# RWKV-7 chain of a hybrid block: more chain work issued per product from its launch on, one pause of 5 instead of 9 products, and the group norm issued in two steps

## The chip, the core and the metric

The kernel runs on one core of one Trainium2 chip. The metric is the device time of one execution in microseconds (us), a median over runs. A core has a matrix engine (TensorE, PE), a vector engine (VectorE, DVE), a scalar engine (ScalarE, ACT), GpSimd (POOL) and a queue engine (SyncE, SP). Each takes its own instructions in the order in which they stand in its program and waits for the others through semaphores. Here SP issues the loads of the weights and POOL nearly all other transfers.

## The reference

One block of a hybrid network on 256 tokens of width 2048, in float32. Four branches (a gated linear recurrence a, an attention with forget gates b, a state-space branch c, RWKV-7 d) read a shared input projection; each branch's output of 512 channels goes through its own matrix and is multiplied by a sigmoid gate; the sum goes through an output projection, an MLP with a short convolution, and a last gated projection. Cut to what matters here:

```python
xn = rmsnorm(h, mix_norm[i])
proj = jnp.einsum('bsd,dn->bsn', xn, w_in[i])
...
y_b = forgetting_attention_branch(b_q, b_k, b_v, b_f, ...)
y_d = rwkv7_branch(d_u, rwkv_mu[i], ...)
gates = jax.nn.sigmoid(g_raw.astype(jnp.float32)).reshape(Bsz, S, N_BRANCH, D)
merged = gates[:, :, 0] * jnp.einsum('bsc,cd->bsd', branches[0], w_branch[i, 0])
for j in range(1, N_BRANCH):
    merged = merged + gates[:, :, j] * jnp.einsum('bsc,cd->bsd', branches[j], w_branch[i, j])
```

and of `rwkv7_branch`, the recurrence over tokens and the group norm behind it:

```python
def step(state, inp):
    r_t, w_t, k_t, v_t, kk_t, a_t = inp
    sa = jnp.einsum('bhvk,bhk->bhv', state, -kk_t)
    state = (state * w_t[:, :, None, :] + sa[..., None] * (kk_t * a_t)[:, :, None, :]
             + v_t[..., None] * k_t[:, :, None, :])
    return state, jnp.einsum('bhvk,bhk->bhv', state, r_t)
...
mean = jnp.mean(y, axis=-1, keepdims=True)
var = jnp.mean(jnp.square(y - mean), axis=-1, keepdims=True)
y = (y - mean) * lax.rsqrt(var + RWKV_LN_EPS) * ln_w.reshape(H, N) + ln_b.reshape(H, N)
```

## The kernel before, in words

**The products.** Every large product is made in units of 256 output columns (`gemm_fm`). The weights of a unit come in chunks of 128 x 1024 numbers. A chunk is loaded by SP into `wr`, and split into a high part `wh` (a rounded copy on ACT, L214) and a low part `wl` (the rest, a subtraction on DVE, L215); there are three buffers of each. PE multiplies high by high, high by low and low by high into the banks `pg`. A gate unit takes four chunks of 24 products each, a branch unit one. "Split n" below is the n-th split of the program on DVE, "chunk n" the products that use it.

**The phases.** After the input projections (through split 96) come the gates and the branch matrices in the order a, c, b, d: for each of a, c and b eight rounds of a gate unit and a branch unit (40 splits); then eight gate units of d (splits 217 to 248), and last eight branch units of d. Gate products are evacuated on DVE (`sb<-pg,R` or `s<-pg,R`, L100), since the banks `pg` are four.

**The chains.** The small computations of the branches are Python generators (`lru`, `ssd`, `fox`, `rwkv`), which issue a step and yield. After the products of each group of a chunk `gemm_fm` calls `pump` (through `hook`), which takes the next step of the oldest live chain while it has credit: each call adds RATE (0.5, in units of us of DVE work), up to three times that; a step costs STEP plus the estimated DVE time of its instructions; and a step that yields a number n costs n times RATE more, so it pauses the chain for n calls. Before a branch unit needs a chain's output, what is left of that chain is issued at once (`drain`).

**The order.** Instructions carry priorities: the weights' splits and evacuations first, then the chains, then the large products (`lane`, with the PE instructions of the chains placed DELAY behind the current product, `on_pe`, L135; other PE instructions are L132). A list scheduler, which runs when the program is built, turns priorities and the order of issue into one fixed order for each engine.

**Places that the prediction names.** The *fox gains* (in `fox`, L120 `sb<-sb,gain,e`) multiply q and k by a norm that went through DRAM (`fox_rn`) to be copied to all partitions. The *key norm* of `rwkv` takes the same way (`rw_kn`). The *triangular solve* of `rwkv` is a loop of 31 multiplications and reductions on DVE (L930); its result goes to DRAM (`rw_q`) and back into `qat` and `qbd`, and the pause behind it is at L947. Two sets of 32 small solve products follow (`pb<-qat,ltb`, `pb<-qbd,xt`), then four *state blocks* (c = 0 to 3), each a row of steps that go back and forth between PE (transposes, 64x64 products) and ACT (copies L986, L1002, L1016). The *group norm* centres and squares y, takes the reciprocal of the variance (L124), and goes through DRAM (`rw_gn`).

Of the kernel before, what the change touches and what calls it, by code (L numbers as in the profile page):

```python
# [19 lines left out]

DELAY, RATE, STEP = 16, 0.5, 0.2
D_FF = 5632
NF = D_FF // P
IN_COLS = 14092
# [59 lines left out]
def body(tc, T, out, dbg=None):  # L86
# [39 lines left out]
    def act(o, i, f, **kw):  # L126
        A.activation(o, i, f, **kw)  # L127
# [23 lines left out]
    def lane(name):  # L151
        prio[cur[0]] = tc.cur_priority
        cur[0] = name
        tc.cur_priority = prio[name]
# [16 lines left out]
    def bank():  # L171
        return psB.tile([P, 512], F32, name="pb", tag="pb")
# [9 lines left out]
    def bslot(dt=F32):  # L182
        return slot(dt, bp)
# [147 lines left out]
    def mm2(o, l, src, start=True, stop=True, pool=sp):  # L331

        h, lo = split_act(src, pool=pool)
        mm(o, l, h, start=start, stop=False)
        mm(o, l, lo, start=False, stop=stop)
# [470 lines left out]
    def rwkv():  # L806
# [136 lines left out]
        for hb in range(4):  # L943
            bs = slice(hb * 32, hb * 32 + 32)
            dq.dma_start(qbd[bs, :, (hb % 2) * 32:(hb % 2) * 32 + 32],
                         bass.AP(tensor=q_d.tensor, offset=q_d.offset + hb * 16 * 1024, ap=blk))
        yield 9  # L947
        px = bank()
        for i in range(16):
            for h in (1, 0):  # L950
# [80 lines left out]
        for j in range(4):  # L1031
            pt = bank()
            mm2(pt[:, :S], center, yT[:, j], pool=bp)
            o = bslot()
            A.copy(o, pt[:, :S])
            yc.append(o)
            yield
        for j in range(4):
            s = bslot()
            act(s, yc[j], AF.Square)  # L1040
            mm2(pr[:8, :S], selR[:, j], s, j == 0, j == 3, bp)
            yield
        w = [bslot() for _ in range(3)]
        rstd_of(w[0][:8], pr[:8, :S], 64.0, 64e-5, w[1][:8], w[2][:8])
        nbc = head_bcast(bcast_rows(w[0][:8], 8, "rw_gn"))
# [41 lines left out]

    active = []

    credit = [0.0]  # L1090

    def pump():

        credit[0] = min(credit[0] + RATE, 3 * RATE)
        if not active or credit[0] <= 0:
            return
        was = cur[0]
        lane("b")
        cost[0] = STEP
        g = active[0]  # L1100
        try:
            credit[0] -= RATE * (next(g) or 0)
        except StopIteration:
            active.remove(g)
        credit[0] -= cost[0]
        lane(was)
# [7 lines left out]
    def proj(name, u0, n):  # L1114
        raw[name] = []
        for u in range(n):
            gemm_fm(T["w_p"][u0 + u], xs, evac_raw(raw[name]))
# [3 lines left out]
    def launch(name, f):  # L1121
        gens[name] = f()
        active.append(gens[name])
# [28 lines left out]
    launch("b", fox)  # L1152
    proj("du", 12, 7)
    launch("d", rwkv)


    merged = [None] * KD
# [230 lines left out]
```

## Time and profile before

| what | before |
|---|---|
| median of 3 runs | 1732.07 us (1731.74 to 1732.73) |
| the profiled execution | 1731.33 us |
| its span, first to last instruction | 1729.4 us |
| mean granted clock of PE in it | 0.999 |
| DVE, share of the span | 71% |
| ACT, share of the span | 55% |
| chain of RWKV in it: first solve products at | 603.9 us |
| chain of RWKV in it: reciprocal of the group norm at | 705.0 us |

The page of a profile gives the busy time of each engine; the timeline gives instructions in order of time with the idle time ahead of them in brackets and what ended it; a table by windows gives the busy time of each engine, with the count of its instructions, for stretches of time. Times are in us from the start of the span. Matmuls overlap in the pipeline, so a PE that is always busy still has a pace, which is told by how many products start in a window.

### The profile page before, as it was taken

What the parts mean: (1) busy time and instruction counts of PE and PEld (TensorE: products, weight loads), DVE (VectorE), ACT (ScalarE), POOL (GpSimd) and SP (SyncE); (2) the same over time, 40 slices, a digit from 0 to 9 for tenths busy, and PEclk for the clock granted to TensorE, in tenths of its full rate; (3) what the DMA queues carried; (4) which work ended last, traced back from release to release, by engine and by line L of the source; (5) the groups of instructions that cost most, each with busy time, mean ns of one, the idle gap of its engine ahead of it and who ended that gap; (6) DMA issues with size and microseconds to landing.
All of it is one profiled execution on the core that took longest, in us unless ns stands there. A gap on an engine that the chain in (4) does not pass through costs nothing.

```text
span 1729.4 us, 29615 instructions
## 1 busy us (share of the span) xinstructions
PE 1713.1 (99%) x11555; PEld 1558.2 (90%) x11555; DVE 1235.8 (71%) x2006; ACT 946.1 (55%) x1426; POOL 92.6 (5%) x155
## 2 busy tenths in 40 slices
PE   8999999999999999999999999999999999999998
PEld 7888888999999999999888888888888888888887
DVE  6888768687789744648778777777777755555676
ACT  6676555556644444545556555555555544444454
POOL 1000000002320100000210000000000000000000
PEclk9999999999999999999999999999999999999999
DMA  9556556556775854665766666666656666666564
GB/s 330 172 170 217 170 175 225 184 179 206 207 213 178 256 159 150 180 185 189 249 209 192 186 193 187 191 189 189 192 188 202 211 208 189 195 193 186 179 217 139
DMA packets 99132, 338.36 MB, mean 196 GB/s; under 512 B 12362, under 2 KB 16624, under 8 KB 98736
## 3 DMA queue, kind: packets, MB, share of 16 engines
q1 hardware_dynamic: 90528, 310.94, 57.6%
q0 software_dynamic: 7456, 21.81, 4.3%
q10 hardware_dynamic: 1008, 3.73, 0.5%
q8 instruction: 90, 1.47, 0.3%
q14 instruction: 50, 0.41, 0.1%
HBM read 326.95 MB, written 9.48 MB: 195 GB/s over the span
## 4 chain that ended last, share of the span: by engine, by line
PE 94%; DVE 2%; DMA 2%; issue 1%; ACT 1%; SPq 0%; DVEq 0%; ACTq 0%
PE pg L132 90%; PE pb L135 4%; DVE wl L215 1%; PE pb L132 1%; DMA wr<-in_w_p_dram 1%; DMA cbr<-in_consts_dram 0%; DVE e L100 0%; DMA d<-in_xT_dram 0%; ACT wh L214 0%; DVE e L930 0%; DMA wr<-in_w_ax_dram 0%; DVE s L100 0%; ACT e L127 0%; DVE sb L100 0%; DVE s L120 0%
## 5 line engine op out<-in xcount | busy, mean ns | idle before, releaser
L132 PE MATMUL pg<-x,wh 128*128 128x512 f32 (+1 forms) x4384 | 1170.9, 339 | 5.5 <-DVE sb L100 5.3
L215 DVE TENSOR_TENSOR wl<-wr,wh 128x1024 fp32r<-128x1024 f32 (+1 forms) x592 | 715.5, 1210 | 408.1 <-ACT wh L214 400.5
L214 ACT CAST wh<-wr 128x1024 fp32r<-128x1024 f32 (+1 forms) x592 | 615.7, 1041 | 648.0 <-PE pg L132 495.9
L132 PE MATMUL pg<-x,wl 128*128 128x256 f32 (+1 forms) x3344 | 918.3, 282 | 3.4 <-DVE wl L215 3.4
L132 PEld LDWEIGHTS pg<-x,wh 128*128 128x128 f32 x4384 | 746.7, 188 | 91.2 <-DVE sb L100 3.1
L132 PEld LDWEIGHTS pg<-x,wl 128*128 128x128 f32 (+1 forms) x3344 | 628.8, 188 | 17.4 <-DVE wl L215 5.4
L132 PE MATMUL pg<-f,wh 128*128 128x512 f32 x704 | 243.2, 390 | 0.0
L132 PE MATMUL pg<-f,wl 128*128 128x256 f32 x704 | 195.8, 282 | 0.0
L132 PEld LDWEIGHTS pg<-f,wh 128*128 128x128 f32 x704 | 131.7, 188 | 26.9
L132 PEld LDWEIGHTS pg<-f,wl 128*128 128x128 f32 x704 | 133.0, 189 | 1.0
L132 PE MATMUL pg<-sb,wh 128*128 128x256 f32 x512 | 94.7, 283 | 0.0
L120 DVE SCALAR_TENSOR_TENSOR s<-s,prm 128x255 f32<-128x255 f32 (+1 forms) x176 | 84.1, 478 | 1.7 <-ACT s L127 1.0
L132 PEld LDWEIGHTS pg<-sb,wh 128*128 128x128 f32 x512 | 79.2, 188 | 0.1
L256 ACT COPY s<-pg 128x256 f32<-128x256 f32 x136 | 49.7, 366 | 45.8 <-PE pg L132 45.8
L132 PE MATMUL pg<-sb,wl 128*128 128x256 f32 x256 | 72.5, 284 | 0.0
L100 DVE TENSOR_TENSOR s<-s 128x256 f32<-128x256 f32 (+1 forms) x172 | 70.5, 419 | 1.6 <-ACT s L127 0.4
L127 ACT ACTIVATE s<-s 128x256 f32<-128x256 f32 x140 | 56.6, 413 | 14.9 <-DVE s L100 14.5
L100 DVE TENSOR_TENSOR s<-s,pg 128x256 f32<-128x256 f32 x136 | 56.1, 414 | 8.3 <-ACT s L256 6.6
L127 ACT ACTIVATE s<-s,prm 128x256 f32<-128x256 f32 x88 | 52.4, 596 | 0.7 <-DVE s L100 0.7
L127 ACT ACT_TABLE_LOAD x38 | 48.8, 1283 | 1.8 <-PEq L1378 1.2
L132 PEld LDWEIGHTS pg<-sb,wl 128*128 128x128 f32 x256 | 48.0, 188 | 0.2
L132 PE MATMUL pg<-d,wh 128*128 128x512 f32 x128 | 45.2, 395 | 0.0
(235 smaller groups left out, 1152.3 us busy)
## 6 DMA issues: line engine op xcount, KB each, us to landing
wr<-in_w_up_dram SPq DMA_DIRECT2D x176, 512.0 KB, 4.2
wr<-in_w_g_dram SPq DMA_DIRECT2D x128, 512.0 KB, 3.6
wr<-in_w_down_dram SPq DMA_DIRECT2D x88, 512.0 KB, 4.0
wr<-in_w_p_dram SPq DMA_DIRECT2D x76, 512.0 KB, 3.7
wr<-in_w_branch_dram SPq DMA_DIRECT2D x32, 512.0 KB, 3.7
wr<-in_w_out_dram SPq DMA_DIRECT2D x32, 512.0 KB, 3.8
wr<-in_w_ple_gate_dram SPq DMA_DIRECT2D x32, 512.0 KB, 4.2
wr<-in_w_v_dram SPq DMA_DIRECT2D x8, 512.0 KB, 4.4
```

The costliest lines, as they stand in the source:

```text
L100: V.tensor_tensor(o, a, b, op=op)
L120: V.scalar_tensor_tensor(o, a, s, b, op0=op0, op1=op1)
L127: A.activation(o, i, f, **kw)
L132: return f(*a, **kw)
L135: f(*a, **kw)
L214: A.copy(wh, wr)
L215: V.tensor_tensor(wl, wr, wh.bitcast(F32), op=ALU.subtract)
L256: A.copy(o, pt[:, S:])
```

## The change

The constant RATE stays for everything ahead of the launch of the RWKV chain, and from that launch on `pump` uses 0.7 in place of 0.5, for all live chains (the fox chain is still live then). The pause behind the writes of the solve's result is 5 calls in place of 9. In the group norm the four centring steps are issued as one step, and the four squares as one step.

```diff
-DELAY, RATE, STEP = 16, 0.5, 0.2
+DELAY, RATE, RATE_D, STEP = 16, 0.5, 0.7, 0.2
@@ rwkv, behind the loads of qat and qbd
-        yield 9
+        yield 5
         px = bank()
@@ rwkv, group norm
             A.copy(o, pt[:, :S])
             yc.append(o)
-            yield
+        yield
         for j in range(4):
             s = bslot()
             act(s, yc[j], AF.Square)
             mm2(pr[:8, :S], selR[:, j], s, j == 0, j == 3, bp)
-            yield
+        yield
@@ pump
-    credit = [0.0]
+    credit, rate = [0.0], [RATE]
...
-        credit[0] = min(credit[0] + RATE, 3 * RATE)
+        credit[0] = min(credit[0] + rate[0], 3 * rate[0])
...
-            credit[0] -= RATE * (next(g) or 0)
+            credit[0] -= rate[0] * (next(g) or 0)
@@ behind the projections
     launch("d", rwkv)
+    rate[0] = RATE_D
```

The new source is two lines longer, so its line numbers are one higher from L23 on (L100 is L101, L215 is L216, L132 is L133, L135 is L136). The order of instructions on three places shows what moved.

DVE at the group norm, before: the rows stand in the gate units of branch d, behind split 225; `8x256` are the norm's sums and `sb<-pg,R` evacuates gate products.

```order
L215 TENSOR_TENSOR wl<-wr,wh 128x1024
L116 TENSOR_SCALAR sb<-pb 8x256
L124 RECIPROCAL sb<-sb 8x256
L215 TENSOR_TENSOR wl<-wr,wh 128x1024
L100 TENSOR_TENSOR sb<-pg,R 128x256 x4
L100 TENSOR_TENSOR sb<-sb 8x256
L120 SCALAR_TENSOR_TENSOR sb<-sb 8x256 x2
```

DVE at the group norm, of the change: now between the gate and branch units of branch b, behind split 196.

```order
L216 TENSOR_TENSOR wl<-wr,wh 128x1024
L101 TENSOR_TENSOR s<-pg,R 128x256
L101 TENSOR_TENSOR sb<-sb 128x256 x2
L101 TENSOR_TENSOR s<-pg,R 128x256
L216 TENSOR_TENSOR wl<-wr,wh 128x1024
L121 SCALAR_TENSOR_TENSOR s<-s,pg 128x256
L117 TENSOR_SCALAR sb<-pb 8x256
L101 TENSOR_TENSOR s<-s 128x256
L121 SCALAR_TENSOR_TENSOR s<-s,pg 128x256
L125 RECIPROCAL sb<-sb 8x256
L101 TENSOR_TENSOR s<-s 128x256
L216 TENSOR_TENSOR wl<-wr,wh 128x1024
```

The norm moved ahead by 28 splits, and the evacuations of its neighbourhood stand ahead of the reciprocal.

DVE at the fox gains, before, behind split 96 (`ccol` belongs to the fox chain, `sb<-sb,pg` evacuates the last input projection).

```order
L114 TENSOR_SCALAR ccol<-pb 128x2x4
L215 TENSOR_TENSOR wl<-wr,wh 128x1024 x2
L100 TENSOR_TENSOR sb<-sb,pg 128x256
L437 TENSOR_SCALAR stamp<-wl 128x1
L100 TENSOR_TENSOR sb<-sb,R 128x256
L116 TENSOR_SCALAR gain<-prm,stamp 128x2
L100 TENSOR_TENSOR sb<-sb,pg 128x256
L114 TENSOR_SCALAR gain<-gain 128x1
L120 SCALAR_TENSOR_TENSOR sb<-sb,gain,e 128x256 x4
```

The same place of the change.

```order
L115 TENSOR_SCALAR ccol<-pb 128x2x4
L216 TENSOR_TENSOR wl<-wr,wh 128x1024
L438 TENSOR_SCALAR stamp<-wl 128x1
L117 TENSOR_SCALAR gain<-prm,stamp 128x2
L115 TENSOR_SCALAR gain<-gain 128x1
L121 SCALAR_TENSOR_TENSOR sb<-sb,gain,e 128x256 x4
L216 TENSOR_TENSOR wl<-wr,wh 128x1024
```

The first four gains stand ahead of split 98 now, and ahead of the two evacuations.

PE at the second set of solve products, before: it stands inside a branch unit (`pg<-sb`), and a gate unit follows.

```order
L132 MATMUL pg<-sb,wl 128x256
L135 MATMUL pb<-qbd,xt_412 64x32 x32
L135 MATMUL pb<-cbr,e 64x128 x4
L132 MATMUL pg<-sb,wh 128x256 x2
L132 MATMUL pg<-sb,wl 128x256
```

PE there, of the change: the first row belongs to chunk 180, the end of the first gate unit of branch b, which has the first set of solve products (`pb<-qat,ltb`) behind its ninth product.

```order
L133 MATMUL pg<-x,wl 128x256
L136 MATMUL pb<-qbd,xt_412 64x32 x32
L136 MATMUL pb<-cbr,e 64x128 x4
L136 MATMUL pb<-cbr,e 128x128 x12
L136 MATMUL pb<-sb,e 64x64 x8
L136 MATMUL pb<-sb,qbd 64x64 x8
L136 MATMUL pb<-sb 64x64 x2
```

Then 29 more rows of 64x64 products follow, and, as the first rows of a large product again:

```order
L136 MATMUL pb<-cbr,e 64x128 x4
L136 MATMUL pb<-cbr,e 128x128 x12
L136 MATMUL pb<-sb,e 64x64 x16
L133 MATMUL pg<-sb,wh 128x256 x2
L133 MATMUL pg<-sb,wl 128x256
```

The whole first state block and the transposes and first products of the second stand without a large product between them, ahead of the first branch unit of b.

## Prediction

> **What bounds the kernel now.** First the page's busy shares and its chain, then the waits of TensorE (PE), then a table by windows around the longest of them, then the timeline of VectorE (DVE) there.
>
> ```profile
> PE 1713.1 (99%) x11555; PEld 1558.2 (90%) x11555; DVE 1235.8 (71%) x2006; ACT 946.1 (55%) x1426; POOL 92.6 (5%) x155
> PE 94%; DVE 2%; DMA 2%; issue 1%; ACT 1%; SPq 0%; DVEq 0%; ACTq 0%
> PE pg L132 <- DVE sb L100: 5.3, 3, 2.9
> ```
>
> PE is the bound: all its idle time together is 1729.4 - 1713.1 = 16.3 us, most of it in the first 50 us, which the change doesn't touch. The program does the same work after the change (by my count each engine has as many instructions as before), so the change can only remove or add idle PE time. The row of waits is the one wait that stands inside the stretch of the change.
>
> ```profile
> 700.00:705.00 5.00, 5.00 (x45) 4.80 (x44) 3.31 (x6) 1.81 (x4) 0.00 (x0) 1.00 0.50 183
> 705.00:710.00 5.00, 2.13 (x11) 1.93 (x11) 4.93 (x9) 4.69 (x7) 0.00 (x0) 0.77 0.57 156
> 710.00:715.00 5.00, 5.00 (x40) 5.00 (x39) 0.70 (x2) 1.72 (x4) 2.98 (x6) 0.89 0.31 101
> ...
> 703.05 1.23 DVE L215 TENSOR_TENSOR wl<-wr,wh 128x1024 fp32r<-128x1024 f32 x1 [1.39 <-ACT wh L214]
> 704.54 0.41 DVE L116 TENSOR_SCALAR sb<-pb 8x256 f32<-8x256 f32 x1 [0.27 <-PE pb L135]
> 704.99 1.74 DVE L124 RECIPROCAL sb<-sb 8x256 f32<-8x256 f32 x1
> 706.66 1.15 DVE L215 TENSOR_TENSOR wl<-wr,wh 128x1024 fp32r<-128x1024 f32 x1
> 707.74 1.39 DVE L100 TENSOR_TENSOR sb<-pg,R 128x256 f32<-128x256 f32 x4
> ...
> 500.00:550.00 50.00, 50.00 (x425) 50.00 (x424) 48.27 (x87) 20.87 (x24) 0.00 (x0) 1.00 0.62 190
> ```
>
> In the windows the columns are PE, PE loads, DVE, ACT, POOL, granted clock, DMA. The place is the group norm of the RWKV chain: its reciprocal (1.74 us) and a weight split stand on DVE ahead of four evacuations of gate products, and PE has no free bank. The last row gives PE's undisturbed pace: 50/425 = 0.1176 us a product, so 24 products (one chunk of a gate unit) are 2.82 us. From 705 to 715 PE starts 51 instead of 85: 34 x 0.1176 = **4.0 us** lost, 2.9 of it waiting, the rest at the lower clock right behind (0.77, 0.89).
>
> **The change, part by part.** The chain gets more room in front of each product, so all of it moves ahead: I count the chain's group norm behind weight split 198 instead of 226.
>
> *The group norm.* In the new order the two gate evacuations stand ahead of the reciprocal, and behind it only an addition and the next split. That split comes 1.74 + 0.4 us late, within the lead of splits over PE (703.05 + 1.23 = 704.28 against a PE that used it from about 711). Gain: 4.0 us; bounds 0 (the wait moves along) and 4.3. Late next are the tiles of the norm's broadcast, which only the chain reads.
>
> *The fox gains.* At the higher rate the fox chain's last pause ends one product sooner, so its gains stand ahead of a split that they stood behind.
>
> ```profile
> 285.73 1.23 DVE L215 TENSOR_TENSOR wl<-wr,wh 128x1024 fp32r<-128x1024 f32 x1 [0.71 <-ACT wh L214]
> ...
> 293.07 1.67 DVE L120 SCALAR_TENSOR_TENSOR sb<-sb,gain,e 128x256 f32<-128x256 f32 x4 [1.59 <-DMA e<-fox_rn]
> ...
> 283.92 1.08 POOL L497 DMA_DIRECT2D e<-fox_rn  x2 [2.71 <-issue]
> ...
> DMA to landing us min/median/max: 2.7/7.2/8.6
> ...
> 293.20 0.39 PE L132 MATMUL pg<-x,wh 128*128 128x256 f32 x2
> ```
>
> The last-but-one row is of the three DMAs of fox_rn: the tile's write 2.7, the two broadcasts 7.2 and 8.6. DVE will wait for the first, until 283.92 + 7.2 = 291.1, then do four gains (1.67) and the split (1.23): 294.0. PE comes to that chunk at 293.20 (its start by the count of products) and needs the split at the third product, 293.44. Cost 0.6 us; bounds 0 and 2.0 (landing as late as 8.6).
>
> *The key norm.* The chain waits for a round trip through DRAM, with three splits between asking and using now, against five before.
>
> ```profile
> 391.73 0.54 POOL L493 DMA_DIRECT2D rw_kn<-sb  x1 [23.77 <-DVE sb L120]
> 395.17 2.43 POOL L799 DMA_DIRECT2D d<-rw_kn  x4 [2.90 <-DMA rw_kn<-sb]
> ...
> d<-rw_kn POOLq DMA_DIRECT2D x4, 128.0 KB, 6.1
> ```
>
> The first pair of the four is issued by 395.17 + 0.6 and lands 6.1 later: 401.9, 10.2 us after the first row. Five chunks (14.1 us) covered it; three (8.5, some 9 with the chain's own products) don't. Behind the waiting DVE instruction stand six of the chain and a split; behind that PE. The splits' lead of about 3 us takes most of it; PE also has a product of the chain in its queue that waits for this. Cost 0.5 us; bounds 0 and 1.4.
>
> *The triangular solve and what comes after.* The pause behind the writes of q is 5 instead of 9 products.
>
> ```profile
> 577.96 1.15 DVE L930 TENSOR_REDUCE e<-e 64x31 f32<-64x961 f32 x1
> ...
> 589.04 1.29 POOL L941 DMA_DIRECT2D qat<-rw_q  x2
> ...
> qat<-rw_q POOLq DMA_DIRECT2D x2, 64.0 KB, 7.3
> ...
> 604.47 1.98 PE pb L135 x62
> ```
>
> From the solve's end (579.1) to the landing of the second qat (589.04 + 0.65 + 7.3 = 597.0) are 17.9 us; PE asked at 604, 7 us later, so it was hidden. In the new order the solve's last reduction stands behind split 174, and PE asks for qat 9 products into chunk 180: 6 x 2.82 + 9 x 0.1176 = 18.0 us after it begins chunk 174. In this loop DVE hands its splits over barely in time (48.27 of 50 us busy in the window above). Behind split 174 stand an addition (0.4, as the evacuations are) and the reduction (1.15), so the solve ends 1.5 us after the split and, with some 0.5 us of lead left to the splits, 1.0 us after PE begins that chunk: PE asks 17.0 us after it. Cost 0.9 us; bounds 0 and 3.
>
> Then, in the new order, from chunk 180 on no product of the gates stands between the steps of the first state block, and the branch product behind them waits for splits of the fox output, which stand behind these steps on ACT. Before, each step had products of the gates around it. So PE now waits for ACT at three steps.
>
> ```profile
> 611.61 1.19 ACT L127 ACTIVATE qbd<-pb 32x512 f32<-32x512 f32 x2 [1.42 <-PE pb L135]
> ...
> 613.91 0.75 ACT L1002 COPY sb<-pb 64x256 f32<-64x256 f32 x2 [0.72 <-PE pb L135]
> ...
> L135 PE MATMUL pb<-cbr,e 128*128 128x128 f32 (+1 forms) x56 | 8.0, 274 | 0.0
> ...
> 618.61 0.28 PE L132 MATMUL pg<-x,wh 128*128 128x256 f32 x1
> 618.81 0.33 PE L135 MATMUL pb<-sb,e 64*64 64x64 f32 x2
> 619.07 0.38 PE L132 MATMUL pg<-x,wh 128*128 128x256 f32 x1
> ...
> 620.09 0.37 ACT L986 COPY sb<-pb 128x256 f32<-128x256 f32 x1 [0.66 <-PE pb L135]
> ...
> 622.87 0.68 PE L135 MATMUL pb<-sb,qbd 64*64 64x64 f32 x16
> 623.48 0.38 PE L132 MATMUL pg<-x,wh 128*128 128x256 f32 x1
> ...
> 623.60 0.39 ACT L127 ACTIVATE sb<-pb 128x256 f32<-128x256 f32 x1 [0.15 <-PE pb L135]
> ```
>
> The first step: the 64 passes of the second solve product end 2.2 us after their start (1.98 in the row above for 62, and 0.2 to the end of the last), then ACT's two activations (1.19) and three copies (3 x 0.37): 4.5 us. PE has 16 transposes meanwhile, 2.0 + 16 x 8.0/56 = 4.3 us at most, 3.8 at the least (their starts lie 0.11 apart): 0.4 us idle. The next two: 16 passes are issued in 0.61 us (622.87 to 623.48) but end at 0.68 and more, then one ACT pass of 0.37 to 0.39 and two hand-overs of about 0.1: 0.6 us idle, twice. Cost 1.6 us; bounds 1.2 and 2.2.
>
> *Fewer changes between products.* A change from a gate product to a 64x64 one costs 618.81 - 618.61 = 0.20 us instead of 0.12, and back 0.26 for two passes instead of 0.07 to 0.1. By my count of the orders there are six such pairs fewer: 6 x 0.2 = 1.2 us if all were so; I take half, -0.6; bounds 0 and -1.2.
>
> Sum: -4.0 + 0.6 + 0.5 + 0.9 + 1.6 - 0.6 = **-1.0 us**. The profiled execution took 1731.33 us (its span of 1729.4 and 1.9 around it), 0.7 under the median of 1732.07; the difference put on the median gives 1731.1.
>
> **Rivals.**
>
> *The clock falls in the cluster.* From chunk 180's end some 12 us hold only small products, transposes and three waits. For: a wait of 2.9 us brought the lower clock for about 3.4 us, as the windows show. Against: each wait here is under 1 us, with work between. Price: one such stretch cost 4.0 - 2.9 = 1.1, two 2.2; I take 2: 1733.1.
> [...]
>
> *The q tiles land late (slower).* PE itself stands at the solve product, so each microsecond of a later landing is one of the kernel. A transfer from the same queue right behind qat took 11.7:
>
> ```profile
> DMA to landing us min/median/max: 7.0/7.7/11.7
> ```
>
> (the four state blocks' loads). With 11.7 instead of 7.3 and the lower clock behind a wait that long: -1.0 + 4.4 + 1.1 = +4.5, 1736.6. It decides from a landing about 3.5 us later than 7.3. For: the slack of 7 us is gone. Against: the two qat loads took nearly the same, and as many bytes move as before.
>
> *The norm's wait goes along.* Were another evacuation caught behind the reciprocal, the 4.0 would stay: 1735.1. Against: the new order has them ahead of it.
>
> *All small waits are hidden.* Landings 1 us sooner, and the fewer changes at full worth: -4.0 + 1.2 - 1.2 + 0 = -4.0: 1728.1.
>
> **How the numbers follow.** A measurement tells about 0.2%, 3.5 us, from no change. Forecast 0.5, with its own range 1729 to 1734 (the bounds added with some against others); clock 0.2; q late 0.13; norm stays 0.08; all hidden 0.09. Predicted 1731.1, range 1728.2 to 1736.6. Faster: the last case and a little of the forecast, 0.1. Slower: q late, and the clock together with a late landing, 0.2. Within: 0.7.
>
> **What would show it.** In the new profile: no wait of 2.9 us of PE on an evacuation near 705; PE waiting about 0.6 us for a split near 293, under 1.5 us at the first 64x32 products near 549, and three short waits on ACT in the 12 us behind, with granted clock 1.00. Wrong if the windows there show under 1.00, if that wait is over 3 us, or if PE waits in a place not named here, such as the solve, where DVE has no lead.

## The result, and the profile after

| | median | runs | range |
|---|---|---|---|
| before | 1731.86 us | 20 | 1729.67 to 1734.24 |
| after | 1735.44 us | 20 | 1731.6 to 1741.14 |

The ratio is 1.0022, with a 95% interval from 1.0015 to 1.0029: the change made the kernel slower by 3.6 us, where the prediction had 1 us less. The time lies inside the predicted range of 1728.2 to 1736.6 us, but on the other side of the kernel before. The profiled execution after took 1734.74 us, its span is 1732.8 us: 3.4 more than before.

The page after, the rows of busy time and of the chain that ended last (by engine, by line):

```profile
PE 1712.2 (99%) x11555; PEld 1557.4 (90%) x11555; DVE 1235.4 (71%) x2006; ACT 945.2 (55%) x1426; POOL 92.5 (5%) x155
...
PE 75%; issue 6%; DMA 1%; DVE 1%; POOL 0%; ACT 0%; DVEq 0%; POOLq 0%; ACTq 0%
PE pg L133 74%; PE pb L136 1%; PE pb L133 1%; DMA e<-fox_rn 0%; DMA rw_q<-e 0%; DMA d<-rw_gn 0%; DMA rw_gn<-sb 0%; DVE wl L216 0%; DVE e L101 0%; POOL e L970 0%; ACT e L936 0%; DVE e L931 0%; DVE sb L121 0%; DVE s L101 0%; POOL qat L942 0%
```

The work is the same, and PE is still the bound. The rows of the chain now name three results that go to DRAM and come back: `fox_rn`, `rw_q` and `rw_gn`. The waits of PE between 280 and 760 us (us in total, times, longest), first before (two more are of 0.2), then after:

```profile
PE pg L132 <- DVE sb L100: 2.9, 1, 2.9
```

```profile
PE pg L133 <- DVE wl L216: 2.8, 2, 1.9
PE pb L136 <- DMA qat<-rw_q: 1.9, 1, 1.9
PE pg L133 <- DVE s L101: 1.3, 1, 1.3
PE pb L136 <- ACT sb L987: 0.8, 1, 0.8
PE pb L136 <- ACT sb L128: 0.5, 1, 0.5
PE pb L136 <- ACT sb L1003: 0.4, 1, 0.4
```

The wait of 2.9 us is gone; in its place stand seven, 7.7 us together. The first row after holds two: 0.97 us at the fox gains (294 us) and 1.87 at 647.6. The second place is where the group norm's broadcast is read. DVE there, then POOL, in the timeline after (start, us, then in brackets the idle time ahead and what ended it):

```profile
635.68 0.85 DVE L121 SCALAR_TENSOR_TENSOR sb<-sb 8x256 f32<-8x256 f32 x2
637.10 1.23 DVE L216 TENSOR_TENSOR wl<-wr,wh 128x1024 fp32r<-128x1024 f32 x1 [0.57 <-ACT wh L215]
639.86 1.22 DVE L216 TENSOR_TENSOR wl<-wr,wh 128x1024 fp32r<-128x1024 f32 x1 [1.53 <-ACT wh L215]
...
641.69 0.42 DVE L101 TENSOR_TENSOR s<-pg,R 128x256 f32<-128x256 f32 x1 [0.27 <-PE pg L133]
647.37 0.88 DVE L121 SCALAR_TENSOR_TENSOR sb<-sb,stamp,d 128x256 f32<-128x256 f32 x2 [5.25 <-DMA d<-rw_gn]
648.16 1.22 DVE L216 TENSOR_TENSOR wl<-wr,wh 128x1024 fp32r<-128x1024 f32 x1
...
636.82 0.55 POOL L494 DMA_DIRECT2D rw_gn<-sb  x1 [59.32 <-DVE sb L121]
640.77 2.43 POOL L800 DMA_DIRECT2D d<-rw_gn  x4 [3.40 <-DMA rw_gn<-sb]
```

The norm is ready at 636.53; its trip through DRAM ends at 647.37, 10.8 us later. DVE stands for the last 5.25 of them, and the split behind it ends at 649.38, when PE has been without weights for 1.87 us. The clock then falls (windows after: PE, PE loads, DVE, ACT, POOL, granted clock, DMA share):

```profile
645.00:650.00 5.00, 3.13 (x27) 2.93 (x26) 2.63 (x5) 1.64 (x2) 0.00 (x0) 1.00 0.35 92
650.00:655.00 5.00, 5.00 (x32) 5.00 (x31) 5.00 (x13) 1.54 (x3) 0.55 (x1) 0.66 0.58 166
```

From 645 to 655 the two rows count 59 products instead of 85 (pace 0.1176 us): 26 x 0.1176 = 3.1 us lost. Counted the same way, the group norm lost 4.0 before. Both are some 0.5 us too low, since a window also counts the products that are still running at its start. One window of 20 us around each place holds 134 (before, 703 to 723) and 142 (after, 645 to 665), where the kernel before has 172 from 680 to 700: 4.5 and 3.5 us lost, so the norm now costs about 0.9 less than before either way. Of the loss after, 1.87 us are the wait and the rest the lower clock. The trip itself was much shorter before: DVE's rows there, and the landing times of the five transfers of `rw_gn`,

```profile
709.50 0.86 DVE L120 SCALAR_TENSOR_TENSOR sb<-sb 8x256 f32<-8x256 f32 x2
...
716.27 0.88 DVE L120 SCALAR_TENSOR_TENSOR sb<-sb,stamp,d 128x256 f32<-128x256 f32 x2 [0.39 <-DMA d<-rw_gn]
```

```profile
DMA to landing us min/median/max: 1.6/3.1/3.2
```

against those after:

```profile
DMA to landing us min/median/max: 3.7/5.5/5.9
```

That is 716.27 - 710.36 = 5.9 us from the norm to its reader, against 10.8. Before, PE stood still just ahead of this trip, and few weights were being loaded (DMA share 0.31 from 710 to 715); after, the share was 0.74 from 640 to 645 (windows). That the load makes the trip longer is what the cases suggest; no run changed the load alone. In the three kernels with PE's wait of 2.9 us just ahead of the trip (before, e9, e11, the last two among the experiments below) the shortest of the five landings was 1.6 us and their median 2.9 to 3.2 (the longest of e9 was 5.6, though); in the ten others the shortest was 2.7 to 3.7 and the median 3.7 to 6.2.

### The profile page after: what moved, and what is told of

The parts are those of the page before. It is cut to its first block, busy times and chain, and to the rows that moved or that the text cites. A ratio compares the mean times of both kernels' runs of the same rounds, so it can differ in the third digit from the quotient of the medians.

```text
span 1732.8 us, 29630 instructions
## 1 busy us (share of the span) xinstructions
PE 1712.2 (99%) x11555; PEld 1557.4 (90%) x11555; DVE 1235.4 (71%) x2006; ACT 945.2 (55%) x1426; POOL 92.5 (5%) x155
## 4 chain that ended last, share of the span: by engine, by line
PE 75%; issue 6%; DMA 1%; DVE 1%; POOL 0%; ACT 0%; DVEq 0%; POOLq 0%; ACTq 0%
PE pg L133 74%; PE pb L136 1%; PE pb L133 1%; DMA e<-fox_rn 0%; DMA rw_q<-e 0%; DMA d<-rw_gn 0%; DMA rw_gn<-sb 0%; DVE wl L216 0%; DVE e L101 0%; POOL e L970 0%; ACT e L936 0%; DVE e L931 0%; DVE sb L121 0%; DVE s L101 0%; POOL qat L942 0%
## 5 line engine op out<-in xcount | busy, mean ns | idle before, releaser
L133 PE MATMUL pg<-x,wh 128*128 128x512 f32 (+1 forms) x4384 | 1167.7, 339 | 3.7 <-DVE sb L101 2.4
L216 DVE TENSOR_TENSOR wl<-wr,wh 128x1024 fp32r<-128x1024 f32 (+1 forms) x592 | 715.3, 1209 | 400.8 <-ACT wh L215 393.8
L215 ACT CAST wh<-wr 128x1024 fp32r<-128x1024 f32 (+1 forms) x592 | 615.6, 1041 | 649.9 <-PE pg L133 489.2
L133 PE MATMUL pg<-x,wl 128*128 128x256 f32 (+1 forms) x3344 | 917.6, 282 | 6.1 <-DVE wl L216 6.0
L133 PEld LDWEIGHTS pg<-x,wh 128*128 128x128 f32 x4384 | 746.1, 188 | 88.7 <-issue 3.5
L133 PEld LDWEIGHTS pg<-x,wl 128*128 128x128 f32 (+1 forms) x3344 | 628.6, 188 | 20.5 <-DVE wl L216 8.3
L133 PE MATMUL pg<-f,wh 128*128 128x512 f32 x704 | 243.2, 390 | 0.0
L133 PE MATMUL pg<-f,wl 128*128 128x256 f32 x704 | 195.8, 282 | 0.0
L133 PEld LDWEIGHTS pg<-f,wh 128*128 128x128 f32 x704 | 131.7, 188 | 26.9
L133 PEld LDWEIGHTS pg<-f,wl 128*128 128x128 f32 x704 | 133.0, 189 | 1.0
L133 PE MATMUL pg<-sb,wh 128*128 128x256 f32 x512 | 94.4, 283 | 0.0
L133 PEld LDWEIGHTS pg<-sb,wh 128*128 128x128 f32 x512 | 78.9, 189 | 0.3
L133 PE MATMUL pg<-sb,wl 128*128 128x256 f32 x256 | 71.8, 282 | 0.0
L101 DVE TENSOR_TENSOR s<-s 128x256 f32<-128x256 f32 (+1 forms) x172 | 70.1, 418 | 1.5 <-ACT s L128 0.4
L101 DVE TENSOR_TENSOR s<-s,pg 128x256 f32<-128x256 f32 x136 | 56.1, 414 | 8.2 <-ACT s L257 6.6
L133 PEld LDWEIGHTS pg<-sb,wl 128*128 128x128 f32 x256 | 47.9, 188 | 0.2
L133 PE MATMUL pg<-d,wh 128*128 128x512 f32 x128 | 45.2, 395 | 0.0
```

What stands on the lines that cost most here:

```text
L101: V.tensor_tensor(o, a, b, op=op)
L133: return f(*a, **kw)
L215: A.copy(wh, wr)
L216: V.tensor_tensor(wl, wr, wh.bitcast(F32), op=ALU.subtract)
```

## The experiments

The first theory was that at the higher rate PE and DVE stand at results of a DRAM round trip before these have landed, each place has its own price, and the rate does it. The rivals were that the shorter pause does it, or the norm's two steps, or that a wait removed just moves on to the next step of the chain. Each kernel was timed with the kernel before on the same chip (its median 1731.27 to 1731.84 us, 1731.86 beside the change), so a difference between kernels that were timed in different groups carries up to 0.6 us that is not theirs; e1 to e11 number them in the order in which they ran.

**The parts alone.** The rate alone (e1), shown against the changed kernel:

```diff
-        yield 5
+        yield 9
         px = bank()
...
             yc.append(o)
-        yield
+            yield
...
             mm2(pr[:8, :S], selR[:, j], s, j == 0, j == 3, bp)
-        yield
+            yield
```

> The change with only its rate of 0.7: the pause is 9 again and the norm takes eight steps again. In the order of instructions the 64x32 products on qat stand where the changed kernel has them (behind the same 9 products of the same chunk), the fox gains and the triangular solve too; the state blocks behind them stand up to five chunks later and no longer all in one gap; the norm's broadcast is again used four splits after its reciprocal. Theory (the rate does it: PE and VectorE now stand at three results of a DRAM round trip before these have landed, and the weight splits behind them come late): the waits at the fox gains (0.97 us), in the solve (1.25) and at qat (1.9) stay, the three short waits on ScalarE shrink from 1.6 to about 0.8, the wait at the norm's broadcast (1.9, and about 1.5 of low clock behind it) stays or goes with the load on the DMAs there: 1734.6, and 1731.5 if the last is gone. First rival (the shorter pause costs the time, since it took the slack from qat): no wait at qat, 1731.9 as before. Second rival (the norm in two steps costs it): no wait at the norm's broadcast, 1732.0.

Measured: 1734.94 us, ratio 1.002 (1.001 to 1.003); 1734.6 expected. The longest of its waits:

```profile
PE pg L133 <- DVE wl L216: 3.5, 3, 1.6
PE pb L136 <- DMA qat<-rw_q: 1.4, 1, 1.4
PE pg L133 <- DVE s L101: 1.3, 1, 1.3
```

The first row holds waits of 1.6 us at the fox gains, 1.1 behind the norm's broadcast and 0.7 later. The rate alone brings the loss, and the wait at qat too: in the order a pause of 9 leaves those products where a pause of 5 has them, so at this rate it isn't the pause that places them.

The change without its rate (e2):

```diff
-DELAY, RATE, RATE_D, STEP = 16, 0.5, 0.7, 0.2
+DELAY, RATE, RATE_D, STEP = 16, 0.5, 0.5, 0.2
```

> The change without its rate: 0.5 throughout, pause 5, norm in two steps. In the order the norm's reciprocal stands behind split 224 (226 before, 198 after) and two gate evacuations stand behind the next split instead of four; qat is used two chunks earlier than before. Theory (the rate does it): 1730.5 to 1732.5, as before; the wait of PE at the norm's evacuations is 2.9 us or less. Rival (the pause or the norm's steps cost the time): a wait at qat of 1.9 or at the norm's broadcast of 1.9, 1733.8 to 1735.4.

Measured: 1737.22 us, ratio 1.0034 (1.0021 to 1.0046): slower than the whole change, which neither the theory nor the rival had. One wait does it, and DVE's timeline shows why:

```profile
PE pg L133 <- DVE sb L101: 7.4, 1, 7.4
```

```profile
703.80 0.73 DVE L101 TENSOR_TENSOR sb<-pg,R 128x256 f32<-128x256 f32 x2
...
715.62 0.88 DVE L121 SCALAR_TENSOR_TENSOR sb<-sb,stamp,d 128x256 f32<-128x256 f32 x2 [3.45 <-DMA d<-rw_gn]
...
723.21 1.99 DVE L101 TENSOR_TENSOR sb<-sb 128x256 fp32r<-128x256 f32 x5
725.11 1.41 DVE L101 TENSOR_TENSOR sb<-pg,R 128x256 f32<-128x256 f32 x4
```

Four gate evacuations stand behind the reader of the broadcast and the whole end of the chain. DVE reaches the reader with 3.45 us to wait, and PE gets its banks back only at 725. So it is not only *when* the chain reads, but *which evacuations stand behind it*.

The pause alone (e8, from the kernel before):

```diff
-        yield 9
+        yield 5
```

> The kernel before with the pause behind the writes of q 5 instead of 9, nothing else. By the order the norm in two steps moves only ten rows of VectorE, eight of ScalarE and seven of TensorE beside this one, so theory (the shorter pause puts the reciprocal two splits earlier, the four evacuations come ahead of the broadcast's reader, and the reader then stands at the landing with PE's evacuations behind it): a wait of 5 to 8 us near 718, 1735 to 1738, as with both edits. Rival (the norm in two steps brought that loss): no wait over 3 us there, 1731.5 as before.

Measured: **1727.41 us**, ratio 0.9976 (0.9966 to 0.9985): faster by 0.24%, against the theory and the rival, which had taken the order as nearly the same. It is not. DVE's rows:

```profile
704.03 0.73 DVE L101 TENSOR_TENSOR sb<-pg,R 128x256 f32<-128x256 f32 x2
...
706.67 0.42 DVE L101 TENSOR_TENSOR sb<-pg,R 128x256 f32<-128x256 f32 x1
...
707.37 0.42 DVE L101 TENSOR_TENSOR sb<-pg,R 128x256 f32<-128x256 f32 x1
...
711.17 1.23 DVE L216 TENSOR_TENSOR wl<-wr,wh 128x1024 fp32r<-128x1024 f32 x1 [1.44 <-ACT wh L215]
715.85 0.88 DVE L121 SCALAR_TENSOR_TENSOR sb<-sb,stamp,d 128x256 f32<-128x256 f32 x2 [3.44 <-DMA d<-rw_gn]
```

DVE waits as long for the broadcast (3.44), but four evacuations and two splits are done ahead of it, and PE has no wait between 690 and 760 us. The two evacuations at 706.67 and 707.37, which stood behind the reader in e2, are worth 1737.22 - 1727.41 = 9.8 us. No run moved these two rows alone; e7 below shows the same from the other side. So the theory falls in its first form, in which the rate alone decides: what decides is what stands behind the reader of a late result, and each edit shifts that in its own way.

The norm's steps alone (e9, from the kernel before):

```diff
             yc.append(o)
-            yield
+        yield
...
             mm2(pr[:8, :S], selR[:, j], s, j == 0, j == 3, bp)
-            yield
+        yield
```

> The kernel before with only the group norm in two steps. In the order two rows of VectorE change places and nothing else does. Theory (at that place the norm's products wait for the last state block, not for their turn, so the steps don't set the order): as before, 1731.3 within 1 us, with the wait of 2.9 us near 705. Rival (the steps by themselves bring part of the loss, since the kernel with pause 5 and the norm in two steps took 9.8 us more than the one with pause 5 alone): 1735 or more.

And the changed kernel with these two lines put back (e10):

```diff
             yc.append(o)
-        yield
+            yield
...
             mm2(pr[:8, :S], selR[:, j], s, j == 0, j == 3, bp)
-        yield
+            yield
```

> The changed kernel with the norm in eight steps again (rate 0.7, pause 5). In the order two rows of VectorE differ from the changed kernel. Theory (the steps don't set the order at this rate either): as the changed kernel, 1735.4 within 1 us, with the wait of about 1.9 us near 647. Rival (the norm in two steps costs time here as it does at rate 0.5 with pause 5): 1732 or less, and no wait at the norm's broadcast.

Measured: 1731.49 us, ratio 1.0 (0.9992 to 1.0009), with the wait of 2.9 us still there; and 1734.47 us, ratio 1.0018 (1.0008 to 1.0028), with a wait of 1.6 at the broadcast (its split ends late behind a DVE wait of 4.97). The steps by themselves change the time by 1 us at most in either; only together with pause 5 at rate 0.5 did they put the two evacuations behind the reader.

**The uses later.** The changed kernel, with the norm's broadcast read 8.5 us later (e3):

```diff
         nbc = head_bcast(bcast_rows(w[0][:8], 8, "rw_gn"))
-        yield 6
+        yield 32
```

> The changed kernel with one number altered: the pause behind the request of the norm's broadcast is 32 instead of 6. In the order 32 rows of VectorE and 16 of TensorE move, all near there: the first reader of the broadcast stands behind split 205 instead of 202, 8.5 us later. Theory (VectorE stands at the broadcast, 10.8 us after its request, with a split behind it, and the low clock comes of PE's wait): the wait of 1.87 us near 647 is gone and the clock stays at 1.00 there, all else as in the changed kernel: 1735.4 - 1.9 - 1.5 = 1732.0. Rival (the lead of the splits is used up there in any order, so the wait comes at the next instruction of the chain): 1734.5 to 1735.4, with a wait of over 1 us within 15 us of the old place.

Measured: 1731.52 us, ratio 1.0001 (0.9992 to 1.001): 3.9 us less than the change, 3.4 expected. No wait is left at the norm, and the clock stays at 1.00 there. The longest waits left are

```profile
PE pb L136 <- DMA qat<-rw_q: 2.0, 1, 2.0
PE pg L133 <- DVE wl L216: 1.3, 1, 1.3
PE pg L133 <- DVE s L101: 1.2, 1, 1.2
```

The clock near qat is the surprise. The windows there, of this kernel and then of the changed one:

```profile
550.00:555.00 5.00, 3.01 (x50) 2.84 (x48) 1.23 (x1) 1.05 (x1) 0.00 (x0) 0.77 1.00 350
555.00:560.00 5.00, 5.00 (x51) 4.81 (x50) 0.58 (x2) 1.22 (x3) 0.00 (x0) 0.55 0.45 177
```

```profile
550.00:555.00 5.00, 3.38 (x75) 3.37 (x76) 1.65 (x2) 0.96 (x3) 0.00 (x0) 1.00 1.02 388
555.00:560.00 5.00, 4.65 (x87) 4.14 (x85) 1.65 (x2) 3.77 (x9) 0.00 (x0) 1.00 0.41 125
```

Behind nearly the same wait at qat (2.0 and 1.9 us) the clock fell in one execution (0.77, 0.55) and not in the other.

The changed kernel with q used five chunks later (e4):

```diff
-        yield 5
+        yield 30
         px = bank()
```

> The changed kernel with one number altered: the pause behind the writes of q is 30 instead of 5. In the order the products on qat stand five chunks (14 us) later, the next ones a chunk behind them, and the state blocks have products of the gates between their steps again; the norm's reciprocal stands behind split 211 instead of 198. Theory (1.9 us at qat and 1.6 us at three steps of the first state block are the price of using q early): both waits gone, 1735.4 - 3.5 = 1731.9; lower by up to 3.4 if the norm's broadcast meets less load on the DMAs at its new place, since its use is again four splits behind the reciprocal. Rival (the landing of qat is itself late by more than the pause covers, or PE's waits only move to the later products): a wait of over 1 us at the first products on qat or in the state blocks, 1734 to 1735.4.

Measured: 1731.77 us, ratio 1.0003 (0.9995 to 1.0012): 3.7 us less than the change, 3.5 expected. The waits at qat and on ACT are gone:

```profile
PE pg L133 <- DVE s L101: 2.2, 2, 1.2
PE pg L133 <- DVE wl L216: 1.9, 2, 1.2
```

Of these rows 1.25 and 0.92 us stand at the norm's broadcast, 682 and 686 us.

Both numbers together (e5):

```diff
-        yield 5
+        yield 30
         px = bank()
...
         nbc = head_bcast(bcast_rows(w[0][:8], 8, "rw_gn"))
-        yield 6
+        yield 32
```

> The two numbers of the last two experiments together in the changed kernel: pause 30 behind the writes of q, pause 32 behind the request of the norm's broadcast. In the order the norm's reciprocal stands behind split 211 and the first reader of its broadcast behind split 217, two splits (5.6 us) later than with the first number alone. Theory (each use of a result that comes back through DRAM costs what it stands before the landing, one apart from the other): the run with q used later still had waits of 1.25 and 0.92 us near 682 and 686 at the norm's broadcast; without them 1731.8 - 2.2 = 1729.6. Rival (the lead of the splits has to be paid back once, wherever the chain ends, so that the second number adds nothing to the first): 1731.0 to 1732.0, with a wait of about 1 us or more behind 680.

Measured: 1729.06 us, ratio 0.9988 (0.9979 to 0.9997); 1729.6 expected. The waits at the norm are gone, so the second number still adds its gain to the first.

With the fox chain's last pause at 6 as well (e6):

```diff
             bcast_full(rbc[i], dn, 4 * i, 4)
...
-        yield 5
+        yield 6
```

> The kernel of the experiment before with a third number: the fox chain's last pause is 6 instead of 5, so that its gains stand one split later, as in the kernel before, with one more split between asking and use. The triangular solve ends behind split 177 instead of 174. Theory: the wait at the fox gains (0.97 us in the changed kernel, 0.64 to 1.6 in the four others) falls under 0.2, the rest as in the experiment before: 1729.6 - 0.8 = 1728.8; the wait in the solve (1.25) is left. Rival (what the gains no longer wait for comes at the next step of the chain, as the lead of the splits is small there): no gain over the experiment before, within 0.5 us of it, or a larger wait in the solve.

Measured: 1730.13 us, ratio 0.9993 (0.9984 to 1.0002): 1.1 us more than e5, where the theory had 0.8 less and the rival no change. Its waits:

```profile
PE pg L133 <- DVE wl L216: 1.0, 1, 1.0
PE pg L133 <- DVE s L101: 1.0, 1, 1.0
PE pb L136 <- ACT beb L897: 0.7, 1, 0.7
PE pb L136 <- DVE sb L121: 0.3, 1, 0.3
```

The wait at the gains did not go: the first row stands at 299 us, behind the gains, and is 1.0 us. The theory had taken 0.17 us, that of the kernel before, as what the old order costs there. That one was the exception. With the gains ordered as in the kernel before, e2, e6, e7, e8, e9 and e11 have 1.0, 1.0, 1.0, 1.0, 0.8 and 1.0 us; with the changed kernel's order, the change, e1, e3, e4, e5 and e10 have 0.97, 1.6, 1.3, 0.6, 1.5 and 0.9. So the gains wait for their late landing in either order, and the earlier place costs about 0.3 us more on the mean.

The kernel with the rate back, and the norm's broadcast read later (e7):

```diff
-DELAY, RATE, RATE_D, STEP = 16, 0.5, 0.7, 0.2
+DELAY, RATE, RATE_D, STEP = 16, 0.5, 0.5, 0.2
...
         nbc = head_bcast(bcast_rows(w[0][:8], 8, "rw_gn"))
-        yield 6
+        yield 32
```

> The kernel with the rate back at 0.5 (pause 5, norm in two steps), which took 1737.2 us, with the pause behind the norm's request 32 instead of 6. In the order the first reader of the norm's broadcast stands behind split 232 instead of 228, and two of the gate evacuations ahead of it. There PE waited 7.4 us near 718 for a gate evacuation that stood on VectorE behind the reader of the broadcast and its successors, with the clock at half for 6.8 us, of which some 3.8 lie behind the wait (about 18 products, 1.7 us lost). Theory (the loss of that kernel is the broadcast's landing, not the pause at qat): 1737.2 - 7.4 - 1.7 = 1728.1, the best so far; PE's wait near the reciprocal is at most 0.5, since two evacuations fewer stand behind it than before. Rival (the wait goes along again, now to the evacuations behind split 230 or to the branch products): 1731.5 or more, with a wait of over 2 us between 700 and 760.

Measured: **1727.07 us**, ratio 0.9976 (0.9967 to 0.9986), 10.2 less than without it; 1728.1 expected. No wait of PE is left between 690 and 760 us.

The later reading in the kernel before (e11):

```diff
         nbc = head_bcast(bcast_rows(w[0][:8], 8, "rw_gn"))
-        yield 6
+        yield 32
```

> The kernel before with the pause behind the norm's request 32 instead of 6: the first reader of the broadcast stands behind split 235 instead of 228; the reciprocal and the split ahead of the four gate evacuations stay as before. Theory (before, PE's 2.9 us come of the reciprocal, 1.74 us, and the split ahead of the four evacuations, not of the broadcast; while PE stands there, the broadcast comes back): the wait of 2.9 us near 705 stays, 1731.3 within 1 us. Rival (the loss at the norm is always the broadcast's, so that its later use brings the gain here too, as it did at rate 0.7 by 3.9 and at rate 0.5 with pause 5 by 10.2): 1727 to 1728.

Measured: 1731.31 us, ratio 1.0 (0.9991 to 1.0009), as the theory had it, with the wait unchanged:

```profile
PE pg L133 <- DVE sb L101: 2.9, 1, 2.9
```

Before, the reciprocal ahead of four evacuations is the loss, and no later reading of the broadcast helps.

## Why the prediction was wrong, point by point

*The group norm (-4.0).* This is the step that failed. The prediction was right that the wait of 2.9 us near 705 goes; it then said: "Late next are the tiles of the norm's broadcast, which only the chain reads." The reader is the chain's, but it stands in DVE's queue, with weight splits behind it, and the sum put nothing for its wait. The trip took 10.8 us instead of 5.9; that PE's wait before had given it a quiet time is suggested by the landings above, not shown. The term measured 3.1 - 4.0 = -0.9, so 3.1 us of the error are here. That they come of reading the broadcast too early is shown: reading it later gave back 3.9. The rival "the norm's wait goes along" had a chance of 0.08, and by another road (an evacuation behind the reciprocal); that its time, 1735.1, was near is luck.

*The solve (no term).* PE waits 1.25 us at 524.6 for an evacuation (`s<-pg,R`) on a DVE that has no lead. The prediction named the place as one that would make it wrong, and gave it no price. In the timeline the evacuation starts at 525.32, behind a multiplication of the solve of 1.74 us, and DVE has no gap from 515 to 528. That this comes of the solve's earlier place is argued: the kernels at rate 0.5 (e2, e7, e8, e9, e11) have no wait over 0.2 us on such an evacuation, but no run moved the solve alone.

*qat (+0.9).* The mechanism was right, the size half of what was measured: 1.91 us. The rows:

```profile
532.13 1.14 DVE L931 TENSOR_REDUCE e<-e 64x31 f32<-64x961 f32 x1
...
543.48 1.29 POOL L942 DMA_DIRECT2D qat<-rw_q  x2 [1.55 <-DMA rw_q<-e]
...
551.62 0.57 PE L136 MATMUL pb<-qat,ltb 64*64 64x32 f32 x11 [1.91 <-DMA qat<-rw_q]
```

The solve ends at 533.27, and the landing is at 551.62, 18.3 us later (17.9 in the sum); PE asked at 551.62 - 1.91 = 549.71, 16.4 us after the solve (17.0 in the sum). Two estimates off by half a microsecond each, in a difference of 0.9. Using q later (e4) took away this wait and those of the next term, 3.5 us together, and gave back 3.7. That the two numbers are so near is in part luck: e4 also moved the norm, which lost less there (64 products from 680 to 690, where 87 or 88 are undisturbed: 2.8 us against 3.5), and brought back the changes between products.

*The state block (+1.6).* Right: 0.38 + 0.76 + 0.48 = 1.62 us on ACT, at 559.7 to 562.6, in the three steps named.

*The fox gains (+0.6)* measured 0.97 against 0.17 before, +0.8 between these two profiles. Most of that is not the change's: over all the kernels the earlier place costs about 0.3 us (see e6). *The key norm (+0.5)* cost nothing: no row of the waits stands there.

*The clock.* "The clock falls in the cluster" (0.2) did not happen in the changed kernel's profile (1.00 in that stretch) but did in those of e1, e3 and e10 (0.78, 0.55 and 0.72 in the lowest windows of 5 us), which use q as early (last section). So some of the change's runs have probably paid it; only one of its 20 executions was profiled.

The sum by these measurements is -0.9 + 1.25 + 1.9 + 1.6 + 0.8 = +4.7, against +3.4 of span; the -1.3 between them is near the bound of the term for fewer changes between products (-0.6, down to -1.2), which no run measured by itself.

One reading of the prediction is off and carries nothing: of PE's 16.3 us of idle time before, 4.9 lie in the first 50 us, 5.4 in the last 30 and 3.3 between 280 and 760.

## What to carry to other kernels

Before a chain is given more room, list each result that it takes through DRAM and ask, for the engine that reads it in order, what stands behind the reader: splits or evacuations there can pay for a late landing (PE waited 1.87 us after the change and 7.4 us in e2; in e8, with two evacuations fewer there, PE has no wait from 690 to 760 us). A landing measured next to a stall may be too short once the stall is gone (from the norm to its reader 5.9 us before, 10.8 after), and one profile is not enough for a wait on a landing: the same order had 0.17 us at the gains in one execution and 0.8 to 1.0 in six others. And where a scheduler decides the order, read it for every variant: two evacuations that changed sides were worth 9.8 us, more than anything the change was made of, and one smaller number alone gave a kernel as fast as any here (0.24% under the kernel before).

## What the runs showed of the hardware

In these traces the granted clock falls behind waits of 1.4 to 2.0 us, and not every time. After the change it was 0.50 from 650.5 to 653.5 us (0.60 in the half microsecond ahead of that, 0.98 in the one behind), behind the wait of 1.87 us, and 1.00 behind the wait of 1.91 us at qat. Before, with the wait of 2.87 us that ended at 708.19, it was 0.50 from 708.0 to 711.0 (0.70 and 0.89 beside that). Behind the wait of 1.4 us in e1 it was 0.88 from 550 to 555 and 0.78 from 555 to 560. The windows of e10, whose waits from 549 to 570 are 1.7 us at qat and then 0.8 or less:

```profile
550.00:555.00 5.00, 3.52 (x73) 3.51 (x74) 1.65 (x2) 1.73 (x3) 0.00 (x0) 0.91 1.01 385
555.00:560.00 5.00, 5.00 (x81) 4.73 (x81) 1.65 (x2) 2.32 (x5) 0.00 (x0) 0.74 0.35 118
560.00:565.00 5.00, 3.38 (x64) 2.77 (x64) 0.00 (x0) 3.07 (x9) 0.00 (x0) 0.94 0.27 99
565.00:570.00 5.00, 5.00 (x81) 4.65 (x79) 0.55 (x2) 2.03 (x6) 0.76 (x1) 0.72 0.15 22
```

These windows give means of 5 us only. Taken at the 0.50 that the finer windows of the two other kernels show, they are by estimate (0.09 + 0.26) x 5 / 0.5 = 3.5 us at half clock, then (0.06 + 0.28) x 5 / 0.5 = 3.4 more; e3 had (0.23 + 0.45) x 5 / 0.5 = 6.8, e1 (0.12 + 0.22) x 5 / 0.5 = 3.4, the norm after the change 0.34 x 5 / 0.5 = 3.4. So in these cases the low clock lasted about 3.4 us or twice that. What sets this length, and why a wait of about 1.9 us (1.87, 1.91 and 2.0 here) sometimes costs it and sometimes not, no run shows.

By the same estimate the second stretch of e10 begins near 564.4, in the window that holds waits of 0.4, 0.8 and 0.5 us on ACT (PE is busy for 3.38 of the 5 us from 560 to 565). Whether these waits brought it is not shown: the same three in the changed kernel (0.38, 0.76 and 0.48 us) and in e3 (0.4, 0.8 and 0.5) brought no low clock there (1.00 from 560 to 570).

The spread of the times goes along in part: with q used early at rate 0.7 the runs lie 5.2 to 9.5 us apart (e1, e3, e10, the change), with q used later 1.4 to 1.7 (e4, e5, e6). But the kernel before, with no wait at qat, spreads by 4.6 to 5.8, so the spread alone doesn't point to this place.
